# Eight heads of values per tile, and the attention branch's merge gates in the later heads

## The chip, the cores and the metric

The kernel runs on one core of a Trainium2 chip. The metric is the device time of one execution in microseconds (us). The kernel before took 881.89 us, the median of three runs from 881.80 to 882.15. A core has five engines that run side by side and wait for each other through semaphores: TensorE (PE: matmuls; its weight loads are shown apart as PEld), VectorE (DVE), ScalarE (ACT), GpSimd (POOL) and SyncE (SP), whose queue issues most of the transfers from memory (DMA). Matmul results land in PSUM, everything else lies in SBUF.

## The reference, cut to what matters

One layer of a hybrid encoder on 512 frames of 1024 features, in float32:

```
xn = rmsnorm(x)
q, k, v, xr, gr, ga, gb = split(xn @ w_in)          # seven parts of 1024 columns
ya = chunked_band_attention(q, k, v, rel_table) @ w_attn_out      # 16 heads of 64
hr = rg_lru(causal_conv(xr))
yb = (hr * gelu(gr)) @ w_rnn_out
h  = x + (sigmoid(ga + b) * ya + sigmoid(gb + b) * yb) @ w_o
h  = h + (silu(g) * up) @ w_ffn_out,   g, up = split(rmsnorm(h) @ w_ffn_in)
out = rmsnorm(h)
```

The change touches the products for `v` and for `ga` (the merge gate of the attention branch).

## The kernel before, in words

**Exactness by splitting.** Every float32 operand is split into a high part (a ScalarE copy to fp32r, line 80) and a low part (a VectorE subtraction, line 81). A product is three matmuls (`mm3`, lines 74 to 76): high by high, high by low, low by high. A tile over all 1024 input features has 8 x 3 = 24 matmuls.

**Weights.** `plan` writes the list of weight chunks in the order of use; one chunk is named after its tiles (`qk3`, `v1`, `ga4`). `load` fetches 128 x 1024 numbers (512 KB) into one of three raw buffers (tag `raw`) on SP's queue. `prefetch` splits them into one of four weight buffers (tag `whl`), or, where `homes` names another place for a chunk, into that one: a buffer of the recurrence (`big`, four of them) or `late`. A narrow chunk of 256 columns needs two weight buffers. `weights(name)` prepares the named chunk and one more ahead. A buffer comes free when the last matmul on it has run.

**Order of work.** First the norm and transposes of x (to about 38 us). Then the recurrence: for each pair of 128-feature blocks j, j+1 the tiles `xr`, `gr` and the gates. All eight `gb` gates are made here and the first four `ga` gates (pairs 0 and 2). Then query and key tile 0, the values of heads 0 to 3 (four tiles of 128 frames by 256 columns), and eight tiles `yb`. Then comes the loop over 16 heads, and after it `ya`, `w_o` and the feed-forward part. Outside the head loop a planner, which simulates the program, orders each engine's instructions. Inside it TensorE's order is as written (`manual_schedule`), and only the other engines' orders are planned.

**A step of the head loop**, head h, on TensorE: the transposes of the probabilities of h (line 677, `pT`); the scores of h+1 (lines 658 and 659, `s`); "before" tiles; the weighing of the values of h (line 697, `o`); "after" tiles. `laid(h)` names the tiles: a query or a key tile before (one pair of heads needs a query tile, a key tile and a step for each), a value tile after in steps 0 to 11, a gate after in step 12 and before in 13 to 15. Step 0 has both tiles of pair 1 before.

**What must be ready.** The softmax of h+1 goes VectorE (bias, minimum: line 662), ScalarE (exponential: line 663), VectorE (reciprocal: line 664), POOL (normalisation: line 666), and the transposes of h+1 wait for it. The bias of a later head is loaded on SP's queue, and POOL writes a corner of it (line 429). A key tile leaves PSUM in four alternating parts per pair (lines 618 to 621: ScalarE, VectorE, ScalarE, and a POOL copy); the scores of the next even head wait for the first half. The weighed head leaves PSUM at lines 698 and 699 (`oacc`), and after each odd head the pair is split (`aT`).

Of the kernel before, what the change touches and what calls it, by code (L numbers as in the profile page):

```python
# [8 lines left out]
F32 = mybir.dt.float32  # L9
# [5 lines left out]
P = 128  # L15
# [21 lines left out]
def block_kernel(ctx: ExitStack, tc: tile.TileContext, x, norm_mix_g, w_in, b_merge, rel_table,  # L37
# [40 lines left out]
    def split(hi, lo, src):  # L78

        act.activation(hi, src, AF.Copy)  # L80
        dve.tensor_sub(lo, src, f(hi))  # L81
# [5 lines left out]
    def cols(src, col, width=CW):  # L87
        return (src, col, width)
# [5 lines left out]
    def plan(name, *parts, rows=0, kts=KT):  # L94
        index[name] = len(chunks)
        chunks.append((name, parts, rows, kts))

    for j in range(0, KT, 2):
        plan(f"xr{j}", cols(w_in, C_XR + j * P))
        plan(f"gr{j}", cols(w_in, C_GR + j * P))  # L100
        if j < 4:
            plan(f"ga{j}", cols(w_in, C_GA + j * P))
        plan(f"gb{j}", cols(w_in, C_GB + j * P))

    def plan_qk(pr):
        plan(f"qk{pr}", cols(w_in, C_Q + pr * P, P), cols(w_in, C_K + pr * P, P))

    def plan_v(gr):
        plan(f"v{gr}", cols(w_in, C_V + gr * CW))

    plan_qk(0)
    plan_v(0)
    for j in range(0, KT, 2):
        plan(f"yb{j}", cols(w_rnn_out, j * P))
    for pr in range(1, HEADS // 2):
# [102 lines left out]
    def prefetch(n):  # L218
        while len(made) < min(n, len(chunks), index.get(barrier[0], len(chunks))):
            name, parts, rows, kts = chunks[len(made)]  # L220
            if name in strassen:
                made.append(weight_sums(name))
                continue
            tiles = []
            wide = sum(width for *_, width in parts)
            step = 4 * CW // wide
            for k in range(0, kts, step):
                n_ = min(step, kts - k)
                if (name, k) in homes:
                    pl, tag, bufs = homes[name, k]  # L230
                    hl = pl.tile([P, 2, n_, wide], F32R, tag=tag, bufs=bufs, name=f"whl_{name}_{k}")
                elif name in extra:
# [3 lines left out]
                if (name, k) not in raws:  # L236
                    load(name, k)
                raw = raws.pop((name, k))
# [5 lines left out]
                tiles.append(hl)  # L244
            made.append(lambda part, k, at, tiles=tiles, step=step: tiles[k // step][:, part, k % step, at])

    def weights(name, ahead=1):
        prefetch(index[name] + 1 + ahead)
# [309 lines left out]
        return po  # L558


    zs = [[zp.tile([P, 2, S], F32, name=f"z{w}{j}") for j in range(0, KT // (1 + (w == "a")), 2)] for w in "ab"]
    ta, zB = ([t[j // 2][:, j % 2] for j in range(2 * len(t))] for t in zs)
# [68 lines left out]

    vs = {}

    def v_tile(gr, t):
        wv = weights(f"v{gr}")
        po = mm_tile(f"po_v{gr}_{t}", "mm" if gr else "t")
        for k in range(KT):
            mm3(po[:, 0:256], xnT[k][:, 0, t * P:(t + 1) * P], xnT[k][:, 1, t * P:(t + 1) * P],
                wv(0, k, whole), wv(1, k, whole), k == 0, k == KT - 1)
        v = aw.tile([P, 2, 4, HD], F32R, tag="v", bufs=8, name=f"v{gr}_{t}")  # L640
        split(v[:, :, 0::3], v[:, :, 1:3], po[:, 0:256].rearrange("p (a b d) -> p a b d", a=2, b=2))
        vs.setdefault(gr, []).append(v)


# [41 lines left out]
    def weigh(h, pp):  # L686
        pr, e = divmod(h, 2)
        own, other = halves(e)
        if e == 0:
            oacc.append(tg_.tile([P, S], F32, tag="tg", name=f"oacc{pr}"))  # L690
        acc = oacc[pr]
        po = mm_tile(f"o{h}")
        for kb in range(NT):
            i, lo, n = ((0, 0, 512), (1, 0, 384), (2, 0, 256), (2, 256, 128))[kb]
            st = vs[pr // 2][kb][:, pr % 2, 2 * e:2 * e + 2].rearrange("p a d -> p (a d)")
            for part in range(2):
                pe.matmul(po[:, S - n:S], st, pp[i][:, part, lo:lo + n], start=kb == 0 and part == 0, stop=kb == NT - 1 and part == 1)  # L697
        act.activation(acc[own, :], po[other, :], AF.Copy)
# [10 lines left out]
    def laid(h):  # L709
        before, after = [], []  # L710
        if h == 0:
            before += [lambda: q_tile(1), lambda: k_tile(1)]
        elif h < 13:
            before.append(lambda: (q_tile if h % 2 else k_tile)(1 + (h + 1) // 2 if h % 2 else 1 + h // 2))
        if h < 12:
            after.append(lambda: v_tile(1 + h // 4, h % 4))
        if h == 12:
            late = zp.tile([P, 2, 2, S], F32, tag="late", bufs=1, name="za_late")
            ta.extend(late[:, i, c] for i in range(2) for c in range(2))
# [281 lines left out]
```

## Time and profile before

| What | Value |
|---|---|
| median of 3 runs | 881.89 us (881.80 to 882.15) |
| the profiled execution | 881.99 us, its span 880.2 us |
| TensorE busy | 869.7 us (99%), 5220 matmuls |
| VectorE, ScalarE, POOL busy | 546.7, 472.4, 111.2 us |
| granted TensorE clock, mean | 0.998 |
| DMA | 90.10 MB, mean 102 GB/s |

All windows and starts in this text are microseconds from the span's start. A row of the timeline is: start, length, engine, line, operation, output tile and inputs, shapes, and in brackets the idle time before it with what ended it. Lengths of matmuls overlap, since they are pipelined; the distance of two starts is what one costs. A row of the chain of waits is: start, length, what ran. In the recurrence and the head loop (39 to 437 us) TensorE's windows are full; in the window from 385 to 397 us, for instance, TensorE is busy for 12.00 us, VectorE 6.85, ScalarE 7.32.

### The profile page before, as it was taken

How to read it: one execution, taken by the hardware profiler on the slowest of the kernel's cores; microseconds unless marked ns; L12 is line 12 of the kernel's file. 1: busy time of each engine (PE TensorE's matmuls, PEld its weight loads, DVE VectorE, ACT ScalarE, POOL GpSimd, SP SyncE). 2: the span in 40 equal slices, each digit the busy share in tenths (PEclk: the TensorE clock that was granted, in tenths of full speed). 3: DMA queues.
4: the chain of work that ended last, by engine and by line, in shares of the span. 5: the costliest groups of instructions: out<-in, count | busy, mean ns of one | idle time of the engine just before them, and what ended most of it. 6: DMA issues, size and time to landing. Idle time of an engine off the chain costs nothing.

```text
span 880.2 us, 13310 instructions
## 1 busy us (share of the span) xinstructions
PE 869.7 (99%) x5220; PEld 776.3 (88%) x5220; DVE 546.7 (62%) x856; ACT 472.4 (54%) x823; POOL 111.2 (13%) x141
## 2 busy tenths in 40 slices
PE   8999999999999999999999999999999999999997
PEld 5988888888888999988888889999999999888886
DVE  5776557663366676665556557888888887554203
ACT  7666656662256776666533366555555555723103
POOL 4013211220011222322100000000000001301100
PEclk9999999999999999999999999999999999999999
DMA  8223232433342232321223630433333332353002
GB/s 268 82 87 98 93 96 81 136 96 95 101 139 74 89 90 83 86 73 60 73 96 114 245 95 27 144 95 121 98 96 99 117 121 73 127 182 121 25 1 96
DMA packets 86079, 90.10 MB, mean 102 GB/s; under 512 B 5376, under 2 KB 74608, under 8 KB 86016
## 3 DMA queue, kind: packets, MB, share of 16 engines
q1 hardware_dynamic: 84640, 85.78, 31.4%
q10 hardware_dynamic: 1376, 3.47, 1.0%
q8 instruction: 41, 0.67, 0.3%
q14 instruction: 22, 0.18, 0.1%
HBM read 87.10 MB, written 2.14 MB: 101 GB/s over the span
## 4 chain that ended last, share of the span: by engine, by line
PE 97%; DVE 1%; ACT 1%; issue 1%; DMA 0%; ACTq 0%
PE po_out L74 5%; PE po_out L76 5%; PE po_out L75 5%; PE p_fg L74 2%; PE o L697 2%; PE p_fg L76 2%; PE p_fu L76 2%; PE p_fu L75 2%; PE p_fg L75 2%; PE p_fu L74 2%; PE pT L677 2%; PE po_v L74 2%; PE po_v L76 2%; PE po_v L75 2%; PE po_ga L74 2%; PE po_q L74 2%
## 5 line engine op out<-in xcount | busy, mean ns | idle before, releaser
L75 PE MATMUL po_out<-whl_fo,act_hi 128*128 128x512 f32 (+1 forms) x198 | 72.5, 366 | 0.0
L74 PE MATMUL po_out<-whl_fo,act_hi 128*128 128x512 f32 (+1 forms) x198 | 72.3, 366 | 0.0
L76 PE MATMUL po_out<-whl_fo,act_lo 128*128 128x512 f32 (+1 forms) x198 | 71.7, 365 | 0.0
L666 POOL TENSOR_SCALAR p<-p,rl 128x128 f32<-128x128 f32 (+1 forms) x64 | 39.7, 638 | 128.8 <-DVE rl L664 128.5
L81 DVE TENSOR_TENSOR whl_fo<-raw_fo,whl_fo 128x1024 fp32r<-128x1024 f32 x22 | 27.8, 1274 | 44.2 <-ACT whl_fo L80 43.8
L885 POOL TENSOR_TENSOR act_lo<-act,act_hi 128x1024 fp32r<-128x1024 f32 x4 | 10.9, 2716 | 323.5 <-ACT act_hi L884 321.5
L80 ACT ACTIVATE whl_fo<-raw_fo 128x1024 fp32r<-128x1024 f32 x22 | 23.0, 1058 | 49.0 <-PE po_out L76 34.6
L663 ACT ACTIVATE p<-p,m 128x128 f32<-128x128 f32 (+1 forms) x64 | 35.8, 560 | 16.1 <-DVE m L662 16.1
L76 PEld LDWEIGHTS po_out<-whl_fo,act_lo 128*128 128x128 f32 x198 | 37.3, 189 | 6.0
L75 PEld LDWEIGHTS po_out<-whl_fo,act_hi 128*128 128x128 f32 x198 | 37.4, 189 | 5.9
L74 PEld LDWEIGHTS po_out<-whl_fo,act_hi 128*128 128x128 f32 x198 | 37.4, 189 | 5.9
L74 PE MATMUL po_v<-whl_v,xnT 128*128 128x256 f32 x128 | 36.8, 287 | 0.0
L76 PE MATMUL po_v<-whl_v,xnT 128*128 128x256 f32 x128 | 36.2, 283 | 0.0
L75 PE MATMUL po_v<-whl_v,xnT 128*128 128x256 f32 x128 | 36.2, 283 | 0.0
L81 DVE TENSOR_TENSOR pp<-pT,pp 128x384 fp32r<-128x384 f32 (+1 forms) x48 | 27.9, 598 | 8.5 <-ACT pp L80 8.5
L662 DVE CUSTOM_DVE_ANT_0 p<-s,bias 128x128 f32<-128x128 f32 (+1 forms) x64 | 29.1, 484 | 0.0
L75 PE MATMUL po_xr<-xnT,whl_xr 128*128 128x512 f32 (+1 forms) x80 | 27.9, 354 | 0.6 <-DVE xnT L362 0.6
L81 DVE TENSOR_TENSOR whl_fg_s<-s_fg,whl_fg_s 128x1024 fp32r<-128x1024 f32 x20 | 25.6, 1294 | 3.7 <-ACT whl_fg_s L80 3.7
L74 PE MATMUL po_gr<-xnT,whl_gr 128*128 128x512 f32 (+1 forms) x80 | 27.8, 349 | 0.1
L76 PE MATMUL po_gr<-xnT,whl_gr 128*128 128x512 f32 (+1 forms) x80 | 27.5, 348 | 0.3 <-DVE whl_gr L81 0.3
L75 PE MATMUL po_gr<-xnT,whl_gr 128*128 128x512 f32 (+1 forms) x80 | 27.6, 347 | 0.0
L81 DVE TENSOR_TENSOR whl_qk<-raw_qk,whl_qk 128x1024 fp32r<-128x1024 f32 x16 | 20.8, 1298 | 10.8 <-ACT whl_qk L80 10.8
(352 smaller groups left out, 3041.1 us busy)
## 6 DMA issues: line engine op xcount, KB each, us to landing
raw_fg<-in_w_ffn_in_dram SPq DMA_DIRECT2D x24, 512.0 KB, 4.1
raw_fu<-in_w_ffn_in_dram SPq DMA_DIRECT2D x22, 512.0 KB, 3.7
raw_fo<-in_w_ffn_out_dram SPq DMA_DIRECT2D x22, 512.0 KB, 4.1
raw_qk<-in_w_in_dram SPq DMA_DIRECT2D x32, 256.0 KB, 3.7
raw_xr<-in_w_in_dram SPq DMA_DIRECT2D x8, 512.0 KB, 4.6
raw_gr<-in_w_in_dram SPq DMA_DIRECT2D x8, 512.0 KB, 3.4
raw_ga<-in_w_in_dram SPq DMA_DIRECT2D x8, 512.0 KB, 3.9
raw_gb<-in_w_in_dram SPq DMA_DIRECT2D x8, 512.0 KB, 3.4
```

Source lines behind the costliest of these rows:

```text
L74: pe.matmul(o, sh, mh, start=start, stop=False, skip_group_check=parts)
L75: pe.matmul(o, sh, ml, start=False, stop=False, skip_group_check=parts)
L76: pe.matmul(o, sl, mh, start=False, stop=stop, skip_group_check=parts)
L80: act.activation(hi, src, AF.Copy)
L81: dve.tensor_sub(lo, src, f(hi))
L662: dve.tensor_tensor_reduce(prob[qb][:], scs[qb], bias[:, S - w:S], -1.0, 3e38, ALU.add, ALU.min, nmax[:, qb:qb + 1])
L663: act.activation(prob[qb][:], prob[qb][:], AF.Exp, bias=nmax[:, qb:qb + 1], scale=-1.0, accum_out=lsum[:, qb:qb + 1])
L666: pool.tensor_scalar(prob[qb][:], prob[qb][:], rl[:, qb:qb + 1], 1.0, ALU.mult, ALU.mult)
L677: pe.transpose(pt[:, at * P:(at + 1) * P], prob[qb][:, kb * P:(kb + 1) * P], ident[:])
L697: pe.matmul(po[:, S - n:S], st, pp[i][:, part, lo:lo + n], start=kb == 0 and part == 0, stop=kb == NT - 1 and part == 1)
L885: (pool if i in (0, 1, 2, 4) else dve).tensor_sub(lo[:], o[:], f(hi[:]))
```

## The change

- The values are made eight heads at a time: two chunks `v0` and `v1` of 512 columns instead of four of 256, so eight tiles with 512 columns instead of sixteen with 256. The tiles of `v1` are in steps 2, 3, 4 (after) and 5 (before) of the head loop. The value buffers (tag `v`, eight) are twice as large.
- A chunk of 512 columns has four pieces of two 128-feature blocks each. Three pieces of `v1` go to the recurrence's buffers (`big`), the last to a weight buffer. For `v0` a place in the value buffers is named for the last two pieces.
- All eight `ga` gates are made in the head loop: after heads 7 to 11, and before the weighing in 13 to 15. Their results lie in value buffers that the first four heads' pairs no longer need. The tiles `za` and `late` go.
- Steps 0, 1, 6 and 12 have nothing after the weighing.
- The list of chunks follows: `v1` comes after `qk2`, the gates from `qk5` on.

```diff
@@ order of the chunks
-        if j < 4:
-            plan(f"ga{j}", cols(w_in, C_GA + j * P))
...
-        plan(f"v{gr}", cols(w_in, C_V + gr * CW))
+        plan(f"v{gr}", cols(w_in, C_V + gr * S, S))
...
-        if pr in (1, 3, 5):
-            plan_v((pr + 1) // 2)
-    for j in (4, 6):
-        plan(f"ga{j}", cols(w_in, C_GA + j * P))
+        for at, what, n in ((2, plan_v, 1), (5, plan_ga, 0), (6, plan_ga, 2), (7, plan_ga, 4), (7, plan_ga, 6)):
+            if pr == at:
+                what(n)
@@ prefetch
-                    pl, tag, bufs = homes[name, k]
-                    hl = pl.tile([P, 2, n_, wide], F32R, tag=tag, bufs=bufs, name=f"whl_{name}_{k}")
+                    pl, tag, bufs, each = homes[name, k]
+                    for i in range(0, n_, each):
+                        hl = pl.tile([P, 2, each, wide], F32R, tag=tag, bufs=bufs, name=f"whl_{name}_{k + i}")
+                        split(hl[:, 0], hl[:, 1], raw[:, i:i + each])
+                        tiles.extend((hl, n) for n in range(each))
+                    continue
@@ places
-    for gr in (1, 2, 3):
-        for k in (0, 4):
-            homes[f"v{gr}", k] = (zp, "late", 1) if (gr, k) == (3, 4) else (rnp, "big", 4)
+    for k in range(0, 6, 2):
+        homes["v1", k] = (rnp, "big", 4, 2)
...
+    for k in (4, 6):
+        homes["v0", k] = (aw, "v", 8, 1)
@@ recurrence
-        for w in range(j // 4, 2):
-            for c in range(2):
-                gate(w, j + c)
+        for c in range(2):
+            gate(1, j + c)
@@ v_tile
-            mm3(po[:, 0:256], xnT[k][:, 0, t * P:(t + 1) * P], xnT[k][:, 1, t * P:(t + 1) * P],
-                wv(0, k, whole), wv(1, k, whole), k == 0, k == KT - 1)
-        v = aw.tile([P, 2, 4, HD], F32R, tag="v", bufs=8, name=f"v{gr}_{t}")
+            mm3(po[:], xnT[k][:, 0, t * P:(t + 1) * P], xnT[k][:, 1, t * P:(t + 1) * P],
+                wv(0, k, every), wv(1, k, every), k == 0, k == KT - 1)
+        v = aw.tile([P, 4, 4, HD], F32R, tag="v", bufs=8, name=f"v{gr}_{t}")
@@ laid
-        if h < 12:
-            after.append(lambda: v_tile(1 + h // 4, h % 4))
-        if h == 12:
...
-            after.append(lambda: gate(0, 4))
-        elif h > 12:
-            before.append(lambda: gate(0, h - 8))
+        if 2 <= h <= 5:
+            (before if h == 5 else after).append(lambda: v_tile(1, h - 2))
+        if h in merged:
+            j = merged.index(h)
+            (before if h > 12 else after).append(lambda: gate_a(j))
         return before, after
+
+    merged = (7, 8, 9, 10, 11, 13, 14, 15)
+
+    def gate_a(j):
+        if j % 2 == 0:
+            za = aw.tile([P, 2, S], F32, tag="v", bufs=8, name=f"za{j}")
+            ta.extend(za[:, c] for c in range(2))
+        gate(0, j)
```

More of the change, by code (lines that the diff above doesn't have):

```diff
@@ L114, in block_kernel, with plan_ga @@
         plan(f"yb{j}", cols(w_rnn_out, j * P))
+    def plan_ga(j):
+        plan(f"ga{j}", cols(w_in, C_GA + j * P))
     for pr in range(1, HEADS // 2):
         plan_qk(pr)
[L117 to L120 removed]
+        for at, what, n in ((2, plan_v, 1), (5, plan_ga, 0), (6, plan_ga, 2), (7, plan_ga, 4), (7, plan_ga, 6)):
+            if pr == at:
+                what(n)
     for j in range(0, KT, 2):
@@ L228, in prefetch @@
                 n_ = min(step, kts - k)
+                if (name, k) not in raws:
+                    load(name, k)
+                raw = raws.pop((name, k))
                 if (name, k) in homes:
-                    pl, tag, bufs = homes[name, k]
-                    hl = pl.tile([P, 2, n_, wide], F32R, tag=tag, bufs=bufs, name=f"whl_{name}_{k}")
-                elif name in extra:
+                    pl, tag, bufs, each = homes[name, k]
[4 more added lines that the diff above has]
+                    continue
+                if name in extra:
                     hl = extra[name].tile([P, 2, n_, wide], F32R, tag="whl", bufs=4, name=f"whl_{name}_{k}")
@@ L235, in prefetch @@
                     hl = wp.tile([P, 2, n_, wide], F32R, tag="whl", bufs=4, name=f"whl_{name}_{k}")
-                if (name, k) not in raws:
-                    load(name, k)
-                raw = raws.pop((name, k))
                 if len(made) == 0 and k:
@@ L243, in prefetch @@
                     split(hl[:, 0], hl[:, 1], raw[:])
-                tiles.append(hl)
-            made.append(lambda part, k, at, tiles=tiles, step=step: tiles[k // step][:, part, k % step, at])
+                tiles.extend((hl, n) for n in range(n_))
+            made.append(lambda part, k, at, tiles=tiles: tiles[k][0][:, part, tiles[k][1], at])
     def weights(name, ahead=1):
@@ L558, in tile_of @@
         return po
-    zs = [[zp.tile([P, 2, S], F32, name=f"z{w}{j}") for j in range(0, KT // (1 + (w == "a")), 2)] for w in "ab"]
-    ta, zB = ([t[j // 2][:, j % 2] for j in range(2 * len(t))] for t in zs)
-    for gr in (1, 2, 3):
-        for k in (0, 4):
-            homes[f"v{gr}", k] = (zp, "late", 1) if (gr, k) == (3, 4) else (rnp, "big", 4)
+    zs = [zp.tile([P, 2, S], F32, name=f"zb{j}") for j in range(0, KT, 2)]
+    ta, zB = [], [zs[j // 2][:, j % 2] for j in range(KT)]
+    for k in range(0, 6, 2):
+        homes["v1", k] = (rnp, "big", 4, 2)
     def gate(w, j):
@@ L637, in v_tile @@
         for k in range(KT):
-            mm3(po[:, 0:256], xnT[k][:, 0, t * P:(t + 1) * P], xnT[k][:, 1, t * P:(t + 1) * P],
-                wv(0, k, whole), wv(1, k, whole), k == 0, k == KT - 1)
-        v = aw.tile([P, 2, 4, HD], F32R, tag="v", bufs=8, name=f"v{gr}_{t}")
-        split(v[:, :, 0::3], v[:, :, 1:3], po[:, 0:256].rearrange("p (a b d) -> p a b d", a=2, b=2))
+            mm3(po[:], xnT[k][:, 0, t * P:(t + 1) * P], xnT[k][:, 1, t * P:(t + 1) * P],
+                wv(0, k, every), wv(1, k, every), k == 0, k == KT - 1)
+        v = aw.tile([P, 4, 4, HD], F32R, tag="v", bufs=8, name=f"v{gr}_{t}")
+        split(v[:, :, 0::3], v[:, :, 1:3], po[:].rearrange("p (a b d) -> p a b d", a=4, b=2))
         vs.setdefault(gr, []).append(v)
```

4 lines of the change are left out of this document (1 added, 3 removed).

## The prediction

> **What bounds the kernel now.** I read the page's busy line and chain first, then who waits for whom on TensorE, then the windows and the timeline of the head loop.
>
> ```profile
> span 880.2 us, 13310 instructions
> PE 869.7 (99%) x5220; PEld 776.3 (88%) x5220; DVE 546.7 (62%) x856; ACT 472.4 (54%) x823; POOL 111.2 (13%) x141
> PE 97%; DVE 1%; ACT 1%; issue 1%; DMA 0%; ACTq 0%
> ```
>
> ```profile
> PE p_fg L74 <- ACT keepa_fg L279: 0.5, 1, 0.5
> PE po_ga L74 <- DVE sp_p L451: 0.3, 1, 0.3
> ```
>
> TensorE is the bound: it is busy 99% of the span and makes 97% of the chain that ended last. The second fence has the only waits of TensorE after 38 us: at 38.9 us (gate tile) and at 558 us (feed-forward). In the stretch that the change touches, the recurrence from 39 us, then attention to 437 us, TensorE never waits. So time goes only with TensorE's own stream, and comes back if that stream now has to wait.
>
> How long a matmul of the stream takes is read from starts, not from durations, which overlap. TensorE's timeline in step 0 of the head loop (start, length):
>
> ```profile
> 250.06 0.40 PE L74 MATMUL po_q<-xnT,whl_qk 128*128 128x512 f32 x1
> 255.54 0.39 PE L74 MATMUL po_k<-xnT,whl_qk 128*128 128x512 f32 x1
> ...
> 262.19 0.33 PE L74 MATMUL po_v<-whl_v,xnT 128*128 128x256 f32 x1
> 262.59 0.28 PE L74 MATMUL po_v<-whl_v,xnT 128*128 128x256 f32 x1
> 262.71 0.28 PE L75 MATMUL po_v<-whl_v,xnT 128*128 128x256 f32 x1
> ...
> 265.11 1.25 PE L677 MATMUL pT<-ident,p 128*128 128x128 f32 x10
> ```
>
> A tile of 24 matmuls with 512 columns takes 255.54 - 250.06 = 5.48 us; a value tile of 24 with 256 columns takes 265.11 - 262.19 = 2.92 us (0.12 each).
>
> **The change, part by part.** *Values.* Sixteen value tiles of 2.92 us become eight of 5.48 us: 46.7 becomes 43.8, a gain of 2.9 us, all on the path. By the two starts alone: a pair of narrow matmuls is 0.24 us, a wide one 5.48/24 = 0.228, so 192 x 0.012 = 2.3 us; the rest is the slower start of each tile (262.19 to 262.59 is three matmuls in 0.40), of which there are eight fewer. I take 2.9.
>
> [...]
>
> Weights are the same bytes: eight loads and eight splits of 128x1024 for the values before and after. What takes the tiles out of PSUM:
>
> ```profile
> L80 ACT ACTIVATE v<-po_v x16: 384/384/385, 194.4 to 396.9; 128x256 fp32r<-128x256 f32 x16
> L81 DVE TENSOR_TENSOR v<-po_v,v x16: 419/425/426, 195.4 to 397.4; 128x256 fp32r<-128x256 f32 x16
> ```
>
> Sixteen of each become eight wider ones, bounded by twice these, off the path.
>
> *Gates.* Four tiles (columns of ga0, ga2) leave the recurrence: 4 x 24 matmuls, 4 tanh on ScalarE, 4 loads on SP, 4 splits (ScalarE copy, VectorE subtraction). All reappear after heads 7 to 10, and the other four move from after 12 and before 13 to 15 to after 11 and before 13 to 15. On SP the loads move past those of the recurrence, yb and qk, and the bias loads; none goes through POOL. For TensorE's stream this is zero. The cover in the recurrence:
>
> ```profile
> 38.91:81.00 42.09, 42.09 (x186) 34.88 (x187) 31.09 (x50) 26.12 (x35) 10.49 (x8) 1.00 0.37 113
> 126.00:160.00 34.00, 34.00 (x151) 28.16 (x151) 23.49 (x28) 21.81 (x29) 7.57 (x6) 1.00 0.27 80
> ```
>
> Columns: window, length, busy PE, PEld, VectorE, ScalarE, POOL. The second window is a pair of blocks that has no such gate already: VectorE 69% and TensorE full. I cost the third pair's pattern for all: zero. The first pair is the exception: without two gate tiles its 42.1 us become 31.1 and VectorE's work, less two splits at 1.32 (row below), 28.5: 92%. Ends: 0, and 2 us if it lags. I take 0.
>
> *Value weights.* The second half of v0 is meant to go to the value buffers, but `homes["v0", ...]` is filled after the first query tile, whose call of `weights` has already prepared v0 (one chunk ahead). So v0 takes all four weight buffers, two of which the first key tile still holds. The last one is free at that tile's end, its split takes 1.05 + 1.32 (rows below), and value tile 0 asks for it after 18 matmuls, 4.1 us. Hidden, 1.3 us to spare; if not, at most one split, 2.4 us. I take 0; no gain is possible here.
>
> *The steps of the head loop* decide. A step is: transposes of head h, scores of h+1, "before" tiles, weighing, "after" tiles. Today steps 0 to 11 have a value tile last; 13 to 15 have nothing last. The chain's transposes that open steps 10, 11 and 12 (length of a step: 11.96 us):
>
> ```profile
> 372.97 1.09 PE pT L677 x10
> 384.94 1.09 PE pT L677 x10
> 396.90 1.09 PE pT L677 x10
> ```
>
> Afterwards 0, 1, 6 and 12 have nothing last, so fewer matmuls cover what must be ready for the next step. TensorE, ScalarE, VectorE and POOL around step 13, which is short already:
>
> ```profile
> 411.32 1.25 PE L677 MATMUL pT<-ident,p 128*128 128x128 f32 x10
> 412.33 0.31 PE L658 MATMUL s<-kh,q 128*128 128x128 f32 x1
> 413.45 0.40 PE L659 MATMUL s<-kl,q 128*128 128x512 f32 x1
> 419.15 1.37 PE L697 MATMUL o<-pp,v 128*128 128x512 f32 x8
> 420.37 0.84 PE L677 MATMUL pT<-ident,p 128*128 128x128 f32 x6
> ```
>
> ```profile
> 412.73 0.69 DVE L81 TENSOR_TENSOR pp<-pT,pp 128x512 fp32r<-128x512 f32 x1 [3.57 <-ACT pp L80]
> 415.30 0.68 DVE L662 CUSTOM_DVE_ANT_0 p<-s,bias 128x512 f32<-128x512 f32 x1
> 416.93 0.18 DVE L664 RECIPROCAL rl<-l 128x4 f32<-128x4 f32 x1 [0.94 <-ACT p L663]
> ```
>
> ```profile
> 417.30 3.01 POOL L666 TENSOR_SCALAR p<-p,rl 128x128 f32<-128x128 f32 x4 [7.47 <-DVE rl L664]
> 427.55 2.06 POOL L666 TENSOR_SCALAR p<-p,rl 128x128 f32<-128x128 f32 x4 [7.23 <-DVE rl L664]
> ```
>
> The softmax ends on POOL at 420.31, the next transposes start at 420.37: it fits with nothing to spare. And VectorE was free when the step began (3.57 us idle). In a short step that follows a key tile it isn't. The end of key tile 7 in step 12, ScalarE and VectorE:
>
> ```profile
> 404.57 1.37 PE L697 MATMUL o<-pp,v 128*128 128x512 f32 x8
> ```
>
> ```profile
> 404.77 0.59 ACT L618 ACTIVATE kh<-po_k 64x512 fp32r<-64x512 f32 x1 [1.58 <-PE po_k L76]
> 405.27 1.05 ACT L80 ACTIVATE whl_ga<-raw_ga 128x1024 fp32r<-128x1024 f32 x1
> 406.34 0.60 ACT L698 ACTIVATE oacc<-o 64x512 f32<-64x512 f32 x1
> 406.96 0.59 ACT L620 ACTIVATE kh<-po_k 64x512 fp32r<-64x512 f32 x1
> ```
>
> ```profile
> 403.22 1.32 DVE L81 TENSOR_TENSOR whl_ga<-raw_ga,whl_ga 128x1024 fp32r<-128x1024 f32 x1 [0.77 <-ACT whl_ga L80]
> 405.40 0.68 DVE L619 TENSOR_TENSOR kl<-po_k,kh 64x512 fp32r<-64x512 f32 x1 [0.86 <-ACT kh L618]
> 406.35 1.49 DVE L81 TENSOR_TENSOR whl_ga<-raw_ga,whl_ga 128x1024 fp32r<-128x1024 f32 x1 [0.27 <-ACT whl_ga L80]
> 408.46 0.69 DVE L619 TENSOR_TENSOR kl<-po_k,kh 64x512 fp32r<-64x512 f32 x1
> ```
>
> The key tile ends at 404.57 and frees a weight buffer, whose split slips in; the keys' second half is ready at 407.55, 2.98 us after. Without an "after" tile the next scores come 1.22 (weighing) + 1.01 (transposes, 412.33 - 411.32) = 2.23 us after: a wait of 0.75. VectorE's last key work ends at 409.15, 4.58 after. Its block of step 13 (412.73 to 415.98, 3.25 us) can then end only at 7.83; POOL ends 4.33 later (420.31 - 415.98), or 3.38 at the 2.06 of the next row: 11.2 to 12.2. The transposes of head 14 are due at 1.22 + 9.05 = 10.27. So steps 12 and 13 together lose 0.95 to 1.9; I take 1.4 (0.75 if VectorE's order is kinder). Steps 0 and 1 are the same place with key tile 1: ends 0 (no split slips in, 1.49 less) and 1.9; I take 0.9. Step 6: its VectorE work of step 5 (output sum, its split, a value tile) now runs into it, as nothing follows the weighing of head 5. Its bounds are step 13's fit (0) and step 4's lateness:
>
> ```profile
> 303.30 0.24 PE s L659
> ```
>
> ```profile
> 309.40 0.15 POOL L429 MEMSET bias<- 64x64 f32 x1 [11.67 <-DMA bias<-ext_d]
> 309.64 3.02 POOL L666 TENSOR_SCALAR p<-p,rl 128x128 f32<-128x128 f32 x4
> ```
>
> From the last score (303.54) to POOL's end (312.66) were 9.12 us, against 6.68 that a short step has (413.69 to 420.37): 2.4. Between 0 and 2.4 I take 0.9, nearer to the clean one, because step 6 itself was clean before.
>
> Sum: -2.9 + 0.9 + 0.9 + 1.4 = +0.3. The profiled execution took 881.99, 0.1 over the median of 881.89; 881.9 + 0.3 = **882.2 us**, no change that a measurement tells (0.2% is 1.8 us).
>
> **Rivals.** *The softmax fits after all, faster.* For it: VectorE is only 62% busy and the planner may put weight splits elsewhere when a step is short; steps 13 and 14 show an exact fit. Against: the key work has nowhere to go. Then only step 12's 0.75 stays: -2.1, 879.8 us.
>
> *POOL stands behind a bias load, slower.* POOL takes its instructions in order, and in step 4 a memset waiting for the bias of a later head (11.67 us) stood ahead of the normalisation. If that order falls on steps 1 and 6, each costs 2.4, with 1.4 at step 12: +3.3, 885.2 us. It decides from the point where the reciprocal comes later than that load is thought to land. The four v1 loads in front of the bias on SP speak for it; against it, step 13's reciprocal follows the last reduction after 0.95 us (415.98 to 416.93).
>
> *The recurrence loses its cover* at the first pair: 2 us, 884.2.
>
> *v0's split comes late*, the half of the change that doesn't do what it says: 2.4 us, 884.6.
>
> [...]
>
> **How the numbers follow.** No change 0.38, the exact fit 0.28, POOL behind a load 0.19, recurrence 0.07, v0 0.05, fixed cost 0.03. Faster is the second, 0.28; slower the last four, 0.34. The likeliest case's own range is 880.2 to 883.6. All stalls at their low ends give 0.75 - 2.9, 879.8; all at the high ends 6.2 - 2.9, 885.2. The range is that with a little for the order that the planner writes anew: 879.2 to 885.6.
>
> **What would show it.** Value tiles: 64 matmuls of 128x512 on each of lines 74 to 76, about 0.228 apart, half of them in steps 2 to 5. Steps: about 14.5 us for 2 to 5 and 7 to 11, 9 to 11 for 1, 6, 13. TensorE's waits: new rows for `s` behind ScalarE's `kh` and for `pT` behind POOL's `p`, 3.2 us together. Wrong if TensorE waits nowhere in the loop (then 879 to 880), or if it waits in the recurrence or behind v0 or yb weights.

## The result, and the profile after

The changed kernel takes 887.39 us (median of six runs, 886.08 to 890.59) against 882.13 us of the kernel before in the same batch (881.80 to 883.05): a ratio of 1.0063, with an interval of 1.0044 to 1.0082. It is slower, by 5.3 us, and lies above the range of the prediction. The profiled execution is the quickest of the six, 886.08 us, with a granted clock of 0.999. The page of the changed kernel, span, busy line of TensorE, and the shares of the chain that ended last:

```profile
span 884.0 us, 12925 instructions
PE 868.4 (98%) x5028; PEld 765.9 (87%) x5028; DVE 548.2 (62%) x848; ACT 469.4 (53%) x815; POOL 108.9 (12%) x141
PE 94%; ACT 2%; DVE 2%; issue 1%; DMA 1%; POOL 0%; DVEq 0%; POOLq 0%; ACTq 0%; SPq 0%
```

There are 192 matmuls fewer, as planned, and TensorE's share of the chain fell from 97% to 94%: other engines now set the end in places. The rows of who waits for whom on TensorE that are new (waiting tile and line, releaser and line, microseconds in total, times, longest):

```profile
PE s L663 <- ACT kh L622: 2.5, 2, 1.9
PE pT L682 <- POOL p L671: 2.3, 4, 1.1
```

These are the two rows that the prediction had named, scores behind the keys and transposes behind POOL's normalisation, with 4.8 us where it expected 3.2. A stop costs 0.2 to 0.3 us more than its wait, as the losses below show (0.8 with a wait of 0.53, 3.1 with four of 2.3 together, 2.2 with one of 1.92). Where they stand is read from the chain of the changed kernel, the starts of the transposes that open a step:

```profile
236.36 1.09 PE pT L682 x10
260.71 1.12 PE pT L682 x10
275.31 1.09 PE pT L682 x10
...
304.46 1.09 PE pT L682 x10
...
345.77 1.09 PE pT L682 x10
...
404.06 1.09 PE pT L682 x10
424.35 1.11 PE pT L682 x10
```

The rows open steps 0, 2, 3, 5, 8, 12 and 14. A step with one tile besides takes 14.57 to 14.60 us (275.31 less 260.71), one without it 9.05, as rows of a later experiment show. Four comparisons follow.

- Step 0 begins at 236.36, in the trace before at 247.86: 11.5 us earlier. Four gates out of the recurrence (4 x 5.48 = 21.9) less what four wider value tiles add (4 x 2.56 = 10.2) make 11.7. TensorE waits for neither the recurrence nor the first half of the values.
- Steps 0 and 1 take 24.35 us. Unhindered they take 23.5, read from the experiment with values in even steps, where they take 20.01 + 9.05 with a wide value tile of 5.5 in them. Lost: 0.8, of which 0.5 is a wait of the scores of head 2 for the keys.
- Steps 5, 6 and 7 take 41.31 us instead of 14.57 + 9.05 + 14.57 = 38.19. Lost: 3.1.
- Steps 12 and 13 take 20.29 us instead of 18.10. Lost: 2.2.

That is 6.1 us lost. After the loop nothing changed.

**Step 6.** Four timelines of the changed kernel (start, length, engine, line, operation, output and inputs, shapes; in brackets the idle time before and its releaser), first VectorE and ScalarE:

```profile
318.86 1.23 DVE L81 TENSOR_TENSOR whl_qk<-raw_qk,whl_qk 128x1024 fp32r<-128x1024 f32 x1 [3.87 <-ACT whl_qk L80]
320.12 0.69 DVE L81 TENSOR_TENSOR v<-po_v,v 128x512 fp32r<-128x512 f32 x1
...
324.14 0.68 DVE L667 CUSTOM_DVE_ANT_0 p<-s,bias 128x512 f32<-128x512 f32 x1
...
325.54 1.22 DVE L81 TENSOR_TENSOR whl_ga<-raw_ga,whl_ga 128x1024 fp32r<-128x1024 f32 x1
326.68 0.17 DVE L669 RECIPROCAL rl<-l 128x4 f32<-128x4 f32 x1
```

```profile
317.77 1.06 ACT L80 ACTIVATE whl_qk<-raw_qk 128x1024 fp32r<-128x1024 f32 x1 [3.51 <-PE po_v L76]
...
324.46 1.05 ACT L80 ACTIVATE whl_ga<-raw_ga 128x1024 fp32r<-128x1024 f32 x1
325.41 0.71 ACT L668 ACTIVATE p<-p,m 128x512 f32<-128x512 f32 x1
```

Then POOL, and TensorE:

```profile
327.98 0.15 POOL L433 MEMSET bias<- 64x64 f32 x1 [15.37 <-DMA bias<-ext_d]
328.23 3.01 POOL L671 TENSOR_SCALAR p<-p,rl 128x128 f32<-128x128 f32 x4
```

```profile
328.65 0.33 PE L682 MATMUL pT<-ident,p 128*128 128x128 f32 x1 [0.64 <-POOL p L671]
330.07 0.33 PE L682 MATMUL pT<-ident,p 128*128 128x128 f32 x1 [1.09 <-POOL p L671]
```

Read it as a relay. ScalarE stood idle for 3.51 us until the last matmul of the last value tile (`po_v`, line 76), and VectorE for 3.87 until ScalarE's half of the split that then began: the query weights' split wanted the weight buffer that the last piece of `v1` held until then. The split, the value tile and the output sum then lay ahead of head 7's softmax. ScalarE ran its half of a gate split ahead of the last exponential and VectorE its half ahead of the reciprocal, which ended at 326.85. POOL could not start then: its queue had the memset, waiting for a bias load, until 327.98. That load was issued at 324.89, right behind the last of the head's reductions on VectorE (324.14 + 0.68), so a late VectorE made it late too. The transposes came between POOL's four pieces.

**Step 12 into 13.** ScalarE, then on TensorE the weighing that follows key tile 7 and the first scores of head 14:

```profile
411.93 1.06 ACT L80 ACTIVATE whl_ga<-raw_ga 128x1024 fp32r<-128x1024 f32 x1 [1.51 <-PE po_k L76]
412.90 0.57 ACT L620 ACTIVATE kh<-po_k 64x512 fp32r<-64x512 f32 x1
413.50 0.59 ACT L703 ACTIVATE oacc<-o 64x512 f32<-64x512 f32 x1
414.11 1.36 ACT L80 ACTIVATE pp<-pT 128x512 fp32r<-128x512 f32 x3
415.50 0.59 ACT L622 ACTIVATE kh<-po_k 64x512 fp32r<-64x512 f32 x1
```

```profile
411.73 1.37 PE L702 MATMUL o<-pp,v 128*128 128x512 f32 x8
...
416.14 0.33 PE L663 MATMUL s<-kh,q 128*128 128x128 f32 x1 [1.92 <-ACT kh L622]
```

The second half of the keys that the scores want is the fifth thing on ScalarE after the key tile: behind a gate split, the first half, the output copy and all three copies of the transposes.

### The profile page after: what moved, and what is told of

Its sections match the earlier page's. It is cut to its first block, busy times and chain, and to the rows that moved or that the text cites. A ratio compares the mean times of both kernels' runs of the same rounds, so it can differ in the third digit from the quotient of the medians.

```text
span 884.0 us, 12925 instructions
## 1 busy us (share of the span) xinstructions
PE 868.4 (98%) x5028; PEld 765.9 (87%) x5028; DVE 548.2 (62%) x848; ACT 469.4 (53%) x815; POOL 108.9 (12%) x141
## 4 chain that ended last, share of the span: by engine, by line
PE 94%; ACT 2%; DVE 2%; issue 1%; DMA 1%; POOL 0%; DVEq 0%; POOLq 0%; ACTq 0%; SPq 0%
PE po_out L74 5%; PE po_out L75 5%; PE po_out L76 5%; PE p_fg L74 2%; PE p_fg L76 2%; PE p_fu L76 2%; PE p_fg L75 2%; PE p_fu L75 2%; PE p_fu L74 2%; PE po_ga L74 2%; PE po_gb L74 2%; PE po_v L74 2%; PE po_q L74 2%; PE po_ga L76 2%; PE po_q L76 2%; PE po_ya L74 2%
## 5 line engine op out<-in xcount | busy, mean ns | idle before, releaser
L75 PE MATMUL po_xr<-xnT,whl_xr 128*128 128x512 f32 (+1 forms) x80 | 27.9, 354 | 0.6 <-DVE xnT L366 0.6
L74 PE MATMUL po_xr<-xnT,whl_xr 128*128 128x512 f32 (+1 forms) x80 | 26.6, 351 | 0.8 <-ACT xnT L365 0.8
L76 PE MATMUL po_xr<-xnT,whl_xr 128*128 128x512 f32 (+1 forms) x80 | 27.3, 346 | 0.0
L81 DVE TENSOR_TENSOR whl_fu_s<-s_fu,whl_fu_s 128x1024 fp32r<-128x1024 f32 x20 | 24.0, 1221 | 4.5 <-ACT whl_fu_s L80 4.5
```

Of the source, the lines that this page charges most:

```text
L74: pe.matmul(o, sh, mh, start=start, stop=False, skip_group_check=parts)
L75: pe.matmul(o, sh, ml, start=False, stop=False, skip_group_check=parts)
L76: pe.matmul(o, sl, mh, start=False, stop=stop, skip_group_check=parts)
```

## The experiments

The theory after the result: step 6 is late because work of step 5 runs over into it, and steps 12 and 13 because a key tile has nothing behind it. The rival for step 6 is POOL's memset behind the load; for the gain, that it comes from the order and not from the width. On the way came one more, that a gap lowers TensorE's granted clock. In each experiment the ratio is to the kernel before, with its median in the same batch beside it.

### Is step 6 late because work runs over from step 5?

The last value tile goes behind the weighing in step 5, so step 5 has work after it.

```diff
-            (before if h == 5 else after).append(lambda: v_tile(1, h - 2))
+            after.append(lambda: v_tile(1, h - 2))
```

> The fourth tile of v1 goes behind the weighing of head 5, not ahead of it; all else is the changed kernel. The changed kernel's step 6 lost 3.2 us. Theory 'work runs over': what step 5 leaves for VectorE and ScalarE is then done under 5.5 us of matmuls before step 6 begins, its softmax takes the usual 6.3 us, and the loss falls below 0.7: profiled execution 883.0 to 883.8 where the changed kernel had 886.1. Rival 'POOL stands behind the bias load': the load starts after step 6's reductions whatever step 5 left, so at least 1.2 us of waiting for it stays: 884.5 to 885.5.

Measured: 887.59 us against 882.65, ratio 1.0051 (1.0036 to 1.0066). Steps 5 to 7 took 42.51 us (305.00 to 347.51), 4.3 lost, of which 1.4 to 1.7 is a lower clock (granted 0.66 in the window 332 to 336, so 0.34 x 4, and 0.91 in the one before, where TensorE was partly idle). The other 2.6 to 2.9 is about what the changed kernel loses. The theory fell: it doesn't matter much on which side of the weighing the tile stands. The rival's range was missed as well, by the lower clock (885.57 is the quickest run). What stayed is that the query split waited for `v1`'s weight buffer and that the memset waited for the bias load, until 328.26.

### Is it the late weight buffer, then?

The tiles of `v1` come one step earlier, so the buffer is free a step earlier; step 5 becomes short instead of step 1.

```diff
-        if 2 <= h <= 5:
-            (before if h == 5 else after).append(lambda: v_tile(1, h - 2))
+        if 1 <= h <= 4:
+            after.append(lambda: v_tile(1, h - 1))
```

> The changed kernel with the tiles of v1 after heads 1 to 4 instead of 2 to 5, so that the weight buffer which v1 holds comes free a step earlier. Theory 'late split': in the changed kernel the split of qk5 waits for that buffer and opens step 6 on VectorE; now it is done in step 5, and step 6's reductions end some 1.2 us earlier, so its loss falls from 3.2 to 1 to 2; step 5, short with a query tile, loses at most 0.5; key tile 1 in step 0 keeps its 0.5: profiled execution 884.3 to 885.5. Rival: step 6 is late from the bias load alone, and keeps 3.2: 886.1.

Measured: 883.90 us against 882.07, ratio 1.0021 (1.0012 to 1.0030). The chain, opening steps 5, 6 and 8:

```profile
310.84 1.09 PE pT L682 x10
319.88 1.12 PE pT L682 x10
...
344.36 1.09 PE pT L682 x10
```

Step 5 loses nothing (9.04), and steps 6 and 7 take 24.48 instead of 9.05 + 14.57 = 23.62: 0.9 lost instead of 3.1. No transposes wait for POOL any more; what waits is a score, 0.41 us, for the keys. Two short steps in a row are no trouble. Three things changed together here: the splits of the query weights are done early in step 5, ScalarE's gate split comes behind the last exponential (325.61, the exponential at 324.89), and the planner put the memset behind the normalisation in step 6 instead of ahead of it (POOL):

```profile
326.14 3.02 POOL L671 TENSOR_SCALAR p<-p,rl 128x128 f32<-128x128 f32 x4 [6.41 <-DVE rl L669]
329.22 0.15 POOL L433 MEMSET bias<- 64x64 f32 x1
```

So this run shows that the place of the value tiles decides, and not how much of it is the buffer. The next one takes the memset alone.

### How much of step 6 is POOL's place behind the load?

Two lasting bias buffers whose corner is written once, so that POOL never waits for a load. Each bias comes in two transfers that leave the corner alone.

```diff
-        b = aw.tile([P, S], F32, tag="bias", bufs=2, name=f"bias{h}")
+        if h < 2:
+            kept.append(aw.tile([P, S], F32, tag=f"bias{h}", bufs=1, name=f"bias{h}"))
+            pool.memset(kept[h][64:128, 448:512], NEG)
+        b = kept[h % 2]
...
-        band = bass.AP(tensor=src.tensor, offset=src.offset, ap=[[1, P], [1, S]])
-        sp.dma_start(out=b[:], in_=band)
-        pool.memset(b[64:128, 448:512], NEG)
+        sp.dma_start(out=b[0:64, :], in_=bass.AP(tensor=src.tensor, offset=src.offset, ap=[[1, 64], [1, S]]))
+        sp.dma_start(out=b[64:128, 0:448], in_=bass.AP(tensor=src.tensor, offset=src.offset + 64, ap=[[1, 64], [1, 448]]))
...
+    kept = []
```

> The changed kernel with two lasting bias buffers: POOL writes their corner once at the start, and each head's load, now two transfers, leaves the corner alone. So POOL never stands behind a bias load. In the changed kernel's step 6 the reciprocal ended at 326.85 and the memset let POOL go at 328.13. Theory 'three delays in a row' (VectorE late by 1.4 us, a weight split of 1.05 + 1.2 ahead of the last exponential and the reciprocal, then 1.3 behind the load): the loss of step 6 falls from 3.2 to 1.9 to 2.2, profiled execution 884.8 to 885.1 at full clock. Rival 'the load is the cause': POOL's order alone made it, the loss falls below 0.7, 883.6 or less.

Measured: 885.75 us against 882.07, ratio 1.0038 (1.0023 to 1.0053). Chain (opening steps 5 and 8) and POOL in step 6:

```profile
304.56 1.09 PE pT L686 x10
344.34 1.09 PE pT L686 x10
```

```profile
327.06 2.06 POOL L675 TENSOR_SCALAR p<-p,rl 128x128 f32<-128x128 f32 x4 [14.65 <-PE po_k L76]
```

Steps 5 to 7 take 39.78, 1.6 us lost instead of 3.1. POOL began 1.2 us earlier than in the changed kernel (327.06 against 328.23, with steps that open within 0.1 us of each other) and took 2.06 instead of 3.01 (the last section has what goes with that). POOL gave 0.5 back: its next copy of the keys took 1.47 us, and a score waited 0.49 for it. So half of step 6 was POOL, by its queue and its pace, and half the lateness of VectorE and ScalarE. Neither theory alone holds. The profiled time, 885.92, missed the range of 884.8 to 885.1 at full clock: behind the stall of step 13 the granted clock was 0.86 and 0.71 from 412 to 420, a shortfall of 1.7 us.

### Steps 12 and 13: a gate put back

The fifth gate goes behind head 12 instead of head 11, so that step 12 has a tile after the weighing and step 11 has none.

```diff
-    merged = (7, 8, 9, 10, 11, 13, 14, 15)
+    merged = (7, 8, 9, 10, 12, 13, 14, 15)
```

> The gate after head 11 goes after head 12; all else is the changed kernel. Steps 12 and 13 lost 2.2 us there, 1.9 of it in the scores of head 14 waiting for key tile 7. Theory 'key tile without cover': that wait is gone, and step 11, short now but without a key tile, loses at most 0.5: profiled execution 883.9 to 884.4 (changed kernel 886.1). Rival 'any short step loses the same': 11 loses what 12 lost, 886.1.

Measured: 885.24 us against 882.65, ratio 1.0031 (1.0019 to 1.0042); its six runs lie at clocks of 0.995 to 0.997. TensorE's scores now wait only so long:

```profile
PE s L663 <- ACT kh L622: 0.5, 1, 0.5
```

The wait of 1.9 is gone, step 6 is as it was (2.3 us behind POOL), and step 11, short now (390.60 to 399.65, 9.05), loses nothing. Step 11 has a query tile where step 12 has a key tile: the stall belongs to a key tile with nothing behind it. By subtraction from the changed kernel's runs at full clock, 886.1 - 2.2, it should have taken 883.9; it took 1.3 more, and this is where the clock came into view.

### The idle time filled

An unused tile of 24 matmuls with 256 columns, 2.9 us, stands after heads 6 and 12: work that the result doesn't need.

```diff
+        if h in (6, 12):
+            after.append(lambda: cover(h))
...
```

> Behind the weighing of heads 6 and 12 TensorE makes one unused tile of 24 matmuls with 256 columns, as long as an old value tile (2.9 us); the result isn't read. All else is the changed kernel. It adds 5.8 us of matmuls where 3.2 + 2.2 us were lost. Theory 'cover': the waits of key tile 7 vanish, and of step 6 what the extra 2.9 us before head 8's scores can't reach stays: step 6's own softmax is due before this tile, so 1.9 to 3.2 stay there only if the tile comes too late for it. With both gone 886.5, with step 6's loss kept 889.5 for the profiled execution. On the clock: the changed kernel's six runs had granted clocks of 0.993 to 0.999 and 886.1 to 890.6 us, slower where lower. If idle TensorE is what lets the clock fall, the runs without long waits stay at 0.998 to 0.999 and within 0.5 us of each other; if the spread has another cause it stays at 3 us and more.

Measured: 886.78 us against 882.65, ratio 1.0052 (1.0035 to 1.0069), and a span of 884.7 against 884.0. TensorE's waits:

```profile
PE s L663 <- ACT kh L622: 0.5, 1, 0.5
PE pT L682 <- POOL p L671: 0.3, 1, 0.3
```

5.8 us of further matmuls cost 0.7 of span. The stalls are time set by other engines, and TensorE could have done that much more in them. Three of the four runs lie at 886.6 to 886.8, one at 888.4 with a clock of 0.996, so filled gaps don't rule out a lower clock altogether.

### Values in even steps: no key tile without something behind it

The tiles of `v1` go after heads 0, 2, 4 and 6, the gates after 8 to 12 and before 13 to 15. What is short is then 1, 3, 5 and 7, all with a query tile. `v1` stands one place earlier in the list of chunks.

```diff
-        for at, what, n in ((2, plan_v, 1), (5, plan_ga, 0), (6, plan_ga, 2), (7, plan_ga, 4), (7, plan_ga, 6)):
+        for at, what, n in ((1, plan_v, 1), (5, plan_ga, 0), (6, plan_ga, 2), (7, plan_ga, 4), (7, plan_ga, 6)):
...
-        if 2 <= h <= 5:
-            (before if h == 5 else after).append(lambda: v_tile(1, h - 2))
+        if h in (0, 2, 4, 6):
+            after.append(lambda: v_tile(1, h // 2))
...
-    merged = (7, 8, 9, 10, 11, 13, 14, 15)
+    merged = (8, 9, 10, 11, 12, 13, 14, 15)
```

> The tiles of v1 follow heads 0, 2, 4 and 6 and the gates heads 8 to 12 (after) and 13 to 15 (before), so that every key tile has a tile of 5.5 us behind it; only steps 1, 3, 5, 7 are short, and none of them has a key tile; v1 is fetched one chunk earlier. Theory 'key tile without cover': no wait behind key tiles, short steps with a query tile lose 0 to 0.5 each: the gain of 2.9 comes out, profiled execution 879.2 to 881. Rival 'any short step loses': four times 0.9 to 3.2, 883 to 892. Rival 'the clock': TensorE waits little, so the runs agree within 0.5 us; if they still spread by 3 us the spread isn't from waits.

Measured: **879.72 us** against 882.65, ratio 0.9966 (0.9953 to 0.9979). It is faster than both kernels. Span on the page, and the chain: the first gate tile of the recurrence, then the transposes that open steps 5 to 8:

```profile
span 877.6 us, 12939 instructions
```

```profile
38.63 0.47 PE po_gb L74
...
303.32 1.09 PE pT L682 x10
312.37 1.11 PE pT L682 x10
326.97 1.09 PE pT L682 x10
336.01 1.12 PE pT L682 x10
```

Steps 5 and 7 are short, 9.05 and 9.04 us, and step 6 with its value tile takes 14.60. No wait of TensorE is left in the loop. The wide value tiles, the gates out of the recurrence and `v0` in the weight buffers are all in this kernel, so with no stall the whole change is worth 2.6 us of span and 2.9 of the median of this batch (2.4 against the 882.07 of the later ones). Of the 2.6, 0.3 lies ahead of the first gate tile, which starts at 38.63 here and at 38.91 in the kernel before; the changed kernel starts it at 38.93, so this part isn't the change's. From that tile on the gain is 2.3.

Then the values in even steps with the gates as the change has them, so that step 12 alone is as in the changed kernel:

```diff
-    merged = (8, 9, 10, 11, 12, 13, 14, 15)
+    merged = (7, 8, 9, 10, 11, 13, 14, 15)
```

> Values after heads 0, 2, 4, 6 as in the even steps, but the gates where the changed kernel has them (after 7 to 11, before 13 to 15): one part of the even arrangement alone. Theory 'key tile without cover': only key tile 7 in step 12 is bare, with the 2.2 us of the changed kernel; steps 0, 4 and 6 lose nothing: profiled execution 881.8 (even steps 879.6), granted clock as in the even steps or a little lower. Rival 'the values' places make no difference': step 6 loses its 3.2 as well, 885.

Measured: 883.46 us against 882.07, ratio 1.0009 (1.0000 to 1.0019). The only wait of TensorE that is left in the loop is that of the scores of head 14 behind the keys, 1.9 us (its row stands further below). One stall costs the whole gain. Its ten runs fall in two groups: two at 882.0, and eight from 883.1 to 884.4. The lower group is 2.3 above the kernel without the stall, which is what steps 12 and 13 lost in the changed kernel (2.2). The profile is of the upper group (883.73), 1.7 above the lower; the granted clock behind the stall, shown further below, accounts for that much.

### What the width alone is worth

Values in even steps, each tile made as two halves of 256 columns in one PSUM tile:

```diff
-        for k in range(KT):
-            mm3(po[:], xnT[k][:, 0, t * P:(t + 1) * P], xnT[k][:, 1, t * P:(t + 1) * P],
-                wv(0, k, every), wv(1, k, every), k == 0, k == KT - 1)
+        for at in (slice(0, CW), slice(CW, S)):
+            for k in range(KT):
+                mm3(po[:, at], xnT[k][:, 0, t * P:(t + 1) * P], xnT[k][:, 1, t * P:(t + 1) * P],
+                    wv(0, k, at), wv(1, k, at), k == 0, k == KT - 1)
```

> The even steps, but each value tile is made as two halves of 256 columns, one after the other, from the same weights into the same PSUM bank: 16 narrow groups of 24 matmuls again, nothing moved. By the starts of the kernel before (2.92 us for 24 narrow, 5.48 for 24 wide) it costs 2.3 to 2.9 us more than the even steps: profiled execution 881.9 to 882.5. [...] Rival 'the gain of the even steps came from the order, not from the width': no change, 879.6.

Measured: 882.26 us against 882.07, ratio 0.9999 (0.9990 to 1.0009). The page's span and, from the chain, the first gate tile:

```profile
span 879.9 us, 13322 instructions
```

```profile
38.78 0.47 PE po_gb L74
```

Narrow costs 2.3 us of span and 2.5 of the median (of another batch). Behind the first gate tile it is 2.2 of the 2.3 that were gained there, so the width is the gain. The starts of a narrow tile's matmuls lie 0.12 apart again (252.22 and 252.34), and the size is the 2.3 that the prediction had from the distance of two starts, within 0.1.

### A gap of TensorE and the clock

Into the kernel with values in even steps, after head 9, where no stall is, goes a chain that leaves TensorE idle: three matmuls, copies on ScalarE, a transpose. Two copies in one kernel, five in the other; none of it is used.

```diff
+        if h == 9:
+            after.append(idle_chain)
...
+    def idle_chain():
+        po = mm_tile("chain")
+        mm3(po[:], xnT[0][:, 0, 0:P], xnT[0][:, 1, 0:P], xnT[0][:, 0], xnT[0][:, 1], True, True)
+        a = tg_.tile([P, S], F32, tag="tg", name="chain_a")
+        act.activation(a[:], po[:], AF.Copy)
+        for _ in range(1):                       # 4 in the other
+            act.activation(a[:], a[:], AF.Copy)
+        pe.transpose(po[:, 0:P], a[:, 0:P], ident[:])
```

> The same with two copies instead of five, so that TensorE idles some 2.4 us, about as long as in step 13 of the changed kernel. 'A gap lets the clock fall, and the longer the likelier': 2.4 + 0.9 us, 882.9, in some runs, and 1 to 2 more in others; a spread of 1 us and more, against 0.5 in the even steps. Rival 'only gaps of 4 us do it': every run within 0.5 us of 882.9 and no window below 0.95.

> The even steps with one gap after head 9: three unused matmuls, five copies on ScalarE one behind the other and an unused transpose that waits for them. In the run of this edit that carried a second, unwanted one TensorE idled 4.3 us there. 'A gap lets the clock fall': 4.3 + 0.9 us at full clock and 1 to 2 more where the clock falls: 885 to 886.8, the window behind the gap at 0.6 to 0.9. Rival: 884.8 in every run and 1.00.

Measured: 883.78 us (ratio 1.0019, 1.0009 to 1.0029) with two copies, 887.15 (1.0057, 1.0042 to 1.0072) with five, before at 882.07. An earlier kernel with five copies (894.86 us) also had two other loops run four times instead of three, so it doesn't compute the layer; nothing rests on it but the 4.3 us of the second expectation. TensorE with two copies:

```profile
369.25 0.33 PE L736 MATMUL chain<-ident,chain_a 128*128 128x128 f32 x1 [2.33 <-ACT chain_a L735]
369.42 2.22 PE L682 MATMUL pT<-ident,p 128*128 128x128 f32 x10
...
372.93 0.40 PE L663 MATMUL s<-kh,q 128*128 128x512 f32 x1
```

The windows of both (window, length, busy PE, PEld, VectorE, ScalarE, POOL, granted clock, DMA share, GB/s), first two copies, then five:

```profile
368.00:372.00 4.00, 2.75 (x14) 2.75 (x15) 1.57 (x3) 2.58 (x6) 0.00 (x0) 0.69 0.68 207
372.00:376.00 4.00, 4.00 (x18) 3.45 (x18) 2.56 (x11) 2.48 (x9) 0.28 (x1) 0.88 0.08 27
```

```profile
372.00:376.00 4.00, 4.00 (x17) 3.81 (x16) 2.79 (x10) 2.65 (x8) 0.00 (x0) 0.50 0.00 0
```

After a gap of 2.33 us ten transposes took 2.22 us instead of the 1.25 that they take in the even steps (at 255.87), and full speed was back at 372.93, 3.7 us after the gap's end: from there the scores of 512 columns start 0.24 us apart, while behind the gap with five copies they start 0.43 apart (374.86 and 375.29). The two windows fall short of full clock by 4 x (0.31 + 0.12) = 1.72 us; at the clock of 0.50 that the window with five copies shows, that would be 3.4 us, by estimate. It doesn't happen in each run. The ten runs with two copies are five from 882.6 to 883.1 with a clock of 0.999 and five from 884.4 to 885.5 with 0.995 to 0.997: some 2 us apart. With five copies the gap and the chain's work alone would give 884.9, and all four runs lie 1.5 to 3.2 above that (886.4 to 888.1). In their profile the fall lasts twice as long, 0.65 and 0.50 in the windows from 368 to 376, part of it while TensorE was idle.

## Why the prediction was wrong

It forecast no change, 882.2 us, and named three stalls of 3.2 us together against a gain of 2.9. The gain came out, at 2.3 to 2.9; the stalls came to 6.1, and a term was missing.

**Right.** *Values, -2.9*: the width is a gain, and without stalls 2.9 of the median came out. But from the first gate tile on the traces show 2.3, the 192 x 0.012 of the prediction; the 0.6 that it added for the slower start of narrow tiles isn't seen. No run shows the "fixed cost" to which the forecast gives a chance of 0.03; what the runs show is starts 0.120 us apart in a narrow tile and 0.228 in a wide one, and 2.3 us more of span with narrow tiles. *Gates moved, 0*, and *`v0` weights, 0*: step 0 begins where the subtraction of the tiles puts it, and two rivals, the recurrence and `v0`, fell with that. (By its own terms `v0` had 4.1 - 2.4 = 1.7 us to spare, not 1.3, which changes nothing.) *Steps 0 and 1, 0.9*: 0.8 lost. The figure is the middle of two bounds, so that it is this close is luck: 0.5 of it is the scores' wait for the keys, which the prediction put at 0.75, and no transposes waited for POOL. POOL's memset stood behind a load in step 0 too, until 245.19, but the normalisation was done at 247.49, ahead of the transposes at 250.68.

**Wrong by size: "Step 6 … I take 0.9, nearer to the clean one, because step 6 itself was clean before."** It lost 3.1. The reason given was no reason: step 6 was clean before with a value tile behind the weighing, which the change takes away. The text had named the output sum, its split and a value tile of step 5 as the late work; what VectorE did first in step 6 was the query weights' split, which the released buffer of `v1` let go only then. With the value tiles a step earlier 0.9 was lost. Its bound of 2.4, from step 4's row, had the memset in it, so the rival "POOL stands behind a bias load" was a true mechanism for one of its two steps; without the memset 1.5 of the 3.1 was gone. How much of the other 1.6 is the query weights' split and how much the gate split was not told apart by a run. The traces give an estimate: from the start of the last reduction to the reciprocal it is 2.54 us in the changed kernel, with the gate split in between, and 1.68 with the value tiles a step earlier, where it comes after (324.10 to 325.78), so some 0.9 is the gate split.

**Wrong by size: "steps 12 and 13 together lose 0.95 to 1.9; I take 1.4."** They lost 2.2. All but 0.3 of it was the scores' wait for the keys, 1.92 us, which the prediction had put at 0.75; the late softmax to which it charged the rest cost nothing more, as the transposes of head 14 didn't wait. The prediction had the keys' second half ready 2.98 us after the key tile, as in the row of before, where a gate tile stood behind the weighing. In the changed kernel it was ready at 416.09, 4.4 us after the weighing began at 411.73, because without that tile the transposes came at once and their three copies went ahead of the keys on ScalarE, 1.36 us. That the planner chose this order because the change moved what is due first is likely; no run shows its reason.

**Missing: the granted clock.** The span comes out without it: 880.2 - 2.3 + 6.1 = 884.0, as in the profiled execution, whose clock is 0.999 (886.08 us). The median of six is 887.39: 1.3 more, at clocks down to 0.993. Idle time of TensorE of some 2 us was followed by a fall of the clock in several profiles of this study. In the kernel with the gates as changed it comes behind the only gap that it has (TensorE's rows, then the window with columns as above):

```profile
412.50 0.47 PE L663 MATMUL s<-kh,q 128*128 128x128 f32 x1 [1.93 <-ACT kh L622]
...
415.01 0.63 PE L74 MATMUL po_ga<-xnT,whl_ga 128*128 128x512 f32 x1
415.44 0.61 PE L75 MATMUL po_ga<-xnT,whl_ga 128*128 128x512 f32 x1
415.87 0.42 PE L76 MATMUL po_ga<-xnT,whl_ga 128*128 128x512 f32 x1
416.12 0.39 PE L74 MATMUL po_ga<-xnT,whl_ga 128*128 128x512 f32 x1
416.35 0.39 PE L75 MATMUL po_ga<-xnT,whl_ga 128*128 128x512 f32 x1
```

```profile
412.00:416.00 4.00, 3.50 (x11) 3.11 (x12) 3.84 (x12) 2.96 (x9) 0.61 (x1) 0.57 0.35 117
```

The gate's matmuls start 0.43 us apart until 415.87, 3.4 us after the gap's end, and 0.23 apart from 416.12. The window is 4 x 0.43 = 1.72 us short of full clock. The same 1.72 comes out of the windows from 412 to 420 with lasting bias buffers, of the made gap of 2.33 us, and of the windows from 328 to 336 with the value tile after head 5 (0.91 and 0.66) and with the gate after head 12 (0.85 and 0.72). The last two stand behind the stall of step 6, which is three or four gaps of at most 1.2 us. In the changed kernel's own profile neither that stall nor the gap of 1.92 us was followed by a fall: its windows are at 1.00.

From 40 to 840 us, 4-us windows under 0.95 (they show 0.50 to 0.91) stood only beside a gap of TensorE, in every profile told of here; the kernels with values in even steps and no gap have none. That such a fall makes the other four runs of the changed kernel longer is likely, but not shown: its profile is of the quickest. A rival is open for part of it: the kernel before, with no gap in the head loop, spreads as well, from 881.77 to 883.43 us at clocks of 1.000 down to 0.996.

## What to carry to other kernels

When a tile is taken out of a step, ask what it covered, and work out the cover anew for the step as it will be: what comes free only when another tile ends, and what the planner will put in front of the next step's work. A tile that the next step needs at its start and that leaves PSUM through a busy engine (here the keys: the scores waited 1.92 us for key tile 7) needs something behind it; one that is wanted only a step later (the queries, which leave by the same engines: step 11 with a query tile and nothing behind it took 9.05 us and lost nothing) can stand last, so where freed work goes is worth as much as the work: the same tiles in even steps turned 5.3 us of loss into 2.9 of gain. A wait for a load should not stand ahead of anything on the path in an engine's queue: in step 6 the reciprocal ended at 326.85, and POOL's normalisation began at 328.23, behind a memset that waited for its bias until 327.98.

## What the runs showed of the hardware that was not expected

- Gaps of TensorE of some 2 us in all, far from idle by the mean, can be followed by some 3.4 us at about half clock (matmuls of 512 columns 0.43 us apart instead of 0.23 until 3.4 us after the gap that ended at 412.50, ten transposes in 2.22 us instead of 1.25, and in each of five profiles windows 1.72 us short in all), in some runs and not in others: the kernel with one stall of 1.9 us has runs at 882.0 and at 883.1 to 884.4, the one with a made gap of 2.3 us at 882.6 to 883.1 and 884.4 to 885.5. Such a stall on TensorE then costs its length and up to 1.7 us more. The rule by which a gap does it isn't known from these runs.
- POOL's normalisation of the same four tiles takes 2.06 us in some steps and 3.01 in others, as the prediction saw. In four traces (before, changed, even steps, lasting bias buffers), each that took 3.0 to 3.1 has the whole of a split by VectorE inside it, and none that took 2.05 to 2.1 has. A short one of the changed kernel, then the VectorE split inside the long one of step 6 (328.23, 3.01 us, shown there):

```profile
310.30 2.06 POOL L671 TENSOR_SCALAR p<-p,rl 128x128 f32<-128x128 f32 x4 [7.48 <-DVE rl L669]
```

```profile
328.42 1.25 DVE L81 TENSOR_TENSOR whl_ga<-raw_ga,whl_ga 128x1024 fp32r<-128x1024 f32 x1 [0.27 <-ACT whl_ga L80]
```

  The two normalisations differ by 0.95 us. No run moved a split for it, so it is a coincidence without exception, not a proof.
